# The order of issue on VectorE, ScalarE and GpSimd, taken from a list scheduler that reads a first trace

## The chip, the core and the metric

The kernel runs on one core of one Trainium2 chip. The metric is the device time of one execution in microseconds (us); a version's time is the median of its runs. The kernel before was run three times: 1061.58, 1067.97 and 1059.37 us, median 1061.58 us.

## The reference

A trunk of two layers on 256 tokens of width 1024, in float32. Each layer has a mixer and a feed-forward part, each followed by a residual sum and a layer norm:

```python
def _layer(x, ...):
    proj = x @ w_in                      # q, k, v, o, gates of branch A; q, k, v, z, gates of branch B; two merge gates
    ha = mlstm_chunked(qa, ka, va, ia, fa)           # 4 heads, exponential gates, running-max stabiliser
    ha = head_rmsnorm(ha) * sigmoid(oa)
    qb, kb, vb = split(silu(causal_conv(qkv_b, conv_w)))     # 4 taps
    hb = gated_delta_chunked(qb, kb, vb, beta, g)    # 8 heads, a unit lower triangular solve in each chunk
    hb = head_rmsnorm(hb) * silu(zb)
    y = sigmoid(gate_a) * (ha @ w_branch_a) + sigmoid(gate_b) * (hb @ w_branch_b)
    x = layernorm(ALPHA * x + y @ w_out)
    gt, up = split(x @ w_ffn_up)
    return layernorm(ALPHA * x + (silu(gt) * up) @ w_ffn_down)
```

## The kernel before

The large products are made from split numbers. A weight tile of 128 x 1024 is loaded to `raw` (three buffers, loads issued by SP, the SyncE queue); ScalarE (ACT) casts it to the high part `wH` (line 232), VectorE (DVE) subtracts to get the low part `wL` (line 233), and TensorE (PE) forms three products for each pair, `wH` x `xtH`, `wH` x `xtL` and `wL` x `xtH` (line 257). `wH` and `wL` have five buffers each, so ScalarE and VectorE can be a few tiles ahead of TensorE. There are some 320 tiles, and they give TensorE nearly all its work. The two numbers behind a tile's name in what follows only tell buffers of one name apart (`wH_876` is made from `raw_878`).

Between these products stand the small parts, all of which put work on VectorE and ScalarE: the gates (`gf`, line 431, to the rows `rw` that are written to DRAM and read back broadcast, lines 494 to 502 and 676), the causal convolutions (`cv`, `cu`, lines 622 to 637), the decay matrices (`KQ`, lines 667 to 725), the scores of branch A (copies `qk`, line 975, matmuls into a `sm` bank), the layer norms (lines 376 to 407) and the triangular solves. A solve is done four times, twice in a layer: VectorE transposes the 32 x 32 diagonal blocks into `Mt` (line 728), runs 31 steps of two operations (`tmp` and `stt`, lines 734 and 736), transposes the result into `t2` (line 740), ScalarE copies it in four pieces into `dm` (line 748), and TensorE multiplies with `dm`.

What sets the order: TensorE's is the order of the code (`manual_schedule` for PE), in which a plan, `PLAN`, tells after which weight tile (`U`) which small part takes its next step. The order of the other engines comes from the framework's own scheduler, by priorities from the place in the code; two places raise a priority by hand (lines 396 and 1027). Within an engine, instructions are issued in that order, and each waits for what it depends on; an instruction that isn't ready holds up those behind it.

Of the kernel before, what the change touches and what calls it, by code (L numbers as in the profile page):

```python
# [1 line left out]

# [8 lines left out]
F32 = mybir.dt.float32  # L11
# [7 lines left out]
NL = 2  # L19
# [111 lines left out]
class Net:  # L131
# [156 lines left out]
        return ps  # L288

    def splitA(self, xt, parts, done, pieces=1, order=None):  # L290
        """For each bank: how many units it has, and how many of them meet both halves of the tokens at once; the
        others meet the first half, and the second half after that of all banks. The last bank's second half is
        accumulated in so many pieces of its columns."""
        work = order or [(n, u) for n in range(len(parts)) for u in range(parts[n][0])]
        ps = {}
        held = []

        def second(n, u, units, us, which):
            cut = pieces if n == len(parts) - 1 else 1
            for i in which(cut):  # L300
                if u == 0:
                    ps[n, 1, i] = self.bank()
                cols = slice(i * 512 // cut, (i + 1) * 512 // cut)
                part = ps[n, 1, i][:, 0:512 // cut]
                self.partA(part, xt, us, u, 1, units - 1, cols=cols)
                if u == units - 1:
                    done(n, 1, part, cols)

        for n, u in work:
            units, both = parts[n]  # L310
            if u == 0:
                ps[n, 0] = self.bank()
            us = self.unit()
            self.partA(ps[n, 0], xt, us, u, 0, units - 1)
            if u < both:
                second(n, u, units, us, range)
                self.free(us)
                self.tick()
            else:
                held.append((n, u, units, us))  # L320
            self.tick()
            if u == units - 1:
                done(n, 0, ps[n, 0], slice(0, 512))
        for i in range(pieces):
            for n, u, units, us in held:
                second(n, u, units, us, lambda cut: (i,) if cut > 1 or i == 0 else ())
                if i == pieces - 1:
                    self.free(us)
                    self.fetch(min(len(self.ahead) + 1, 8))
                self.tick()  # L330
# [786 lines left out]
            self.F = None  # L1117


def program(arrays, dbg_shapes=None):  # L1120
    nc = bacc.Bacc("TRN2", target_bir_lowering=False, num_devices=1)
    a = {n: nc.dram_tensor("in_" + n, v.shape, mybir.dt.from_np(v.dtype), kind="ExternalInput").ap()
         for n, v in arrays.items()}
    out = nc.dram_tensor("out", (S, D), F32, kind="ExternalOutput").ap()
    dbg = None
    if dbg_shapes:
        dbg = {n: nc.dram_tensor("dbg_" + n, s, F32, kind="ExternalOutput").ap() for n, s in dbg_shapes.items()}
    with tile.TileContext(nc) as tc, ExitStack() as ctx:
        with tc.manual_schedule(engines={mybir.EngineType.PE}):
            Net(ctx, tc, a, dbg).run(out)  # L1130
    return nc


# [5 lines left out]
```

## Time and profile before

| | |
|---|---|
| runs | 1061.58, 1067.97, 1059.37 us (median 1061.58) |
| span of the profiled execution | 1058.5 us (only its span is given; the runs lie 0.9 to 9.5 us above it) |
| PE, PEld busy | 97%, 91% |
| DVE, ACT, POOL busy | 69%, 56%, 4% |
| granted TensorE clock, mean | 0.992 |
| chain that ended last | PE 71%, DMA 11%, DVE 8%, ACT 6%, issue 2%, POOL 1% |

PE is TensorE's matmul queue, PEld its weight loads, DVE VectorE, ACT ScalarE, POOL GpSimd, SP SyncE. Times in the views are microseconds from the start of the span. In a timeline, what stands in brackets is the time that the engine sat idle before the row, and what it then waited for. A granted clock of 1.00 is 2.4 GHz, one of 0.50 is 1.2 GHz.

### The profile page before, as it was taken

How to read it: one execution, taken by the hardware profiler on the slowest of the kernel's cores; microseconds unless marked ns; L12 is line 12 of the kernel's file. 1: busy time of each engine (PE TensorE's matmuls, PEld its weight loads, DVE VectorE, ACT ScalarE, POOL GpSimd, SP SyncE). 2: the span in 40 equal slices, each digit the busy share in tenths (PEclk: the TensorE clock that was granted, in tenths of full speed). 3: DMA queues.
4: the chain of work that ended last, by engine and by line, in shares of the span. 5: the costliest groups of instructions: out<-in, count | busy, mean ns of one | idle time of the engine just before them, and what ended most of it. 6: DMA issues, size and time to landing. Idle time of an engine off the chain costs nothing.

```text
span 1058.5 us, 18755 instructions
## 1 busy us (share of the span) xinstructions
PE 1030.0 (97%) x7378; PEld 959.5 (91%) x7378; DVE 730.0 (69%) x1309; ACT 596.7 (56%) x1106; POOL 42.5 (4%) x63
## 2 busy tenths in 40 slices
PE   8998999999999999999999989999999999999997
PEld 6897999989998799998788979999999978999886
DVE  5668976898658655655648598879985785555553
ACT  5567476757555544444535755667566654544441
POOL 0001000100000000000000100001000010000001
PEclk9999999999999999999999999999999999999999
DMA  7755525554456556666635564344544575666661
GB/s 243 260 182 183 170 87 160 159 179 140 140 179 217 178 175 191 197 196 200 221 106 182 159 220 140 119 144 156 161 151 145 183 242 156 185 196 197 188 211 41
DMA packets 57689, 183.62 MB, mean 173 GB/s; under 512 B 6656, under 2 KB 14336, under 8 KB 56960
## 3 DMA queue, kind: packets, MB, share of 16 engines
q1 hardware_dynamic: 50976, 179.13, 53.3%
q10 hardware_dynamic: 6624, 3.28, 1.2%
q8 instruction: 58, 0.95, 0.4%
q14 instruction: 31, 0.25, 0.1%
HBM read 181.21 MB, written 1.18 MB: 172 GB/s over the span
## 4 chain that ended last, share of the span: by engine, by line
PE 71%; DMA 11%; DVE 8%; ACT 6%; issue 2%; POOL 1%; SPq 0%; ACTq 0%; POOLq 0%; DVEq 0%
PE pj L257 61%; DMA raw<-in_ws 9%; PE sm L257 8%; DVE wL L233 3%; ACT wH L232 2%; DMA KQ<-rw 1%; PE sm L367 1%; DMA mr<-rw 1%; PE sm L647 1%; ACT wh L232 1%; DMA rw<-rt 1%; DVE wT L233 1%; POOL lnc L400 0%; DVE x L407 0%; DVE wh L233 0%
## 5 line engine op out<-in xcount | busy, mean ns | idle before, releaser
L233 DVE TENSOR_TENSOR wL<-raw,wH 128x1024 fp32r<-128x1024 f32 (+1 forms) x302 | 366.5, 1216 | 187.9 <-ACT wH L232 186.1
L232 ACT CAST wH<-raw 128x1024 fp32r<-128x1024 f32 (+1 forms) x302 | 315.3, 1046 | 266.5 <-PE pj L257 178.2
L257 PE MATMUL pj<-xtH,wH 128*128 128x256 f32 x1328 | 374.1, 282 | 1.5 <-ACT wH L232 1.5
L257 PE MATMUL pj<-xtH,wL 128*128 128x256 f32 x1328 | 368.9, 278 | 1.5 <-DVE wL L233 1.5
L257 PE MATMUL pj<-xtL,wH 128*128 128x256 f32 x1328 | 368.7, 278 | 0.0
L257 PEld LDWEIGHTS pj<-xtH,wH 128*128 128x128 f32 x1328 | 249.9, 188 | 2.1 <-ACT wH L232 1.9
L257 PEld LDWEIGHTS pj<-xtH,wL 128*128 128x128 f32 x1328 | 249.9, 188 | 2.0 <-DVE wL L233 1.9
L257 PEld LDWEIGHTS pj<-xtL,wH 128*128 128x128 f32 x1328 | 250.1, 188 | 0.1
L257 PE MATMUL pj<-wH,xtH 128*128 128x512 f32 x216 | 75.7, 412 | 2.6 <-ACT wH L232 2.6
L257 PE MATMUL pj<-wH,xtL 128*128 128x512 f32 x216 | 73.3, 400 | 0.0
L257 PE MATMUL pj<-wL,xtH 128*128 128x512 f32 x216 | 72.6, 397 | 0.1
L632 DVE SCALAR_TENSOR_TENSOR cv<-cu,cw,cv 128x255 f32<-128x255 f32 (+2 forms) x144 | 64.2, 480 | 7.3 <-ACT cv L630 6.8
L257 PE MATMUL pj<-wH,hH 128*128 128x512 f32 (+1 forms) x168 | 62.7, 373 | 0.0
L257 PE MATMUL pj<-wL,hH 128*128 128x512 f32 (+1 forms) x168 | 62.5, 372 | 0.0
L257 PE MATMUL pj<-wH,hL 128*128 128x512 f32 (+1 forms) x168 | 62.5, 372 | 0.0
L257 PEld LDWEIGHTS pj<-wH,xtL 128*128 128x128 f32 x216 | 41.7, 193 | 9.6
L257 PEld LDWEIGHTS pj<-wH,xtH 128*128 128x128 f32 x216 | 40.4, 194 | 10.9 <-ACT wH L232 3.5
L257 PEld LDWEIGHTS pj<-wL,xtH 128*128 128x128 f32 x216 | 41.5, 193 | 9.3 <-DVE wL L233 0.5
L734 DVE TENSOR_TENSOR tmp<-Mt,stt 128x248 f32<-128x248 f32 (+30 forms) x124 | 36.0, 290 | 1.7
L736 DVE TENSOR_TENSOR stt<-stt,tmp 128x248 f32<-128x248 f32 (+30 forms) x124 | 36.0, 290 | 1.7
L257 PEld LDWEIGHTS pj<-wH,hL 128*128 128x128 f32 x168 | 31.9, 190 | 5.5
L257 PEld LDWEIGHTS pj<-wH,hH 128*128 128x128 f32 x168 | 32.0, 190 | 5.3
(254 smaller groups left out, 1581.8 us busy)
## 6 DMA issues: line engine op xcount, KB each, us to landing
raw<-in_ws SPq DMA_DIRECT2D x322, 512.0 KB, 4.1
lnp<-in_ln SPq DMA_DIRECT2D x4, 1024.0 KB, 5.1
KQ<-rw ACTq DMA_DIRECT2D x8, 256.0 KB, 5.1
raw<-in_ws SPq DMA_DIRECT2D x4, 256.0 KB, 4.2
gn<-in_gn SPq DMA_DIRECT2D x2, 512.0 KB, 5.6
x<-in_x SPq DMA_DIRECT2D x1, 1024.0 KB, 8.2
mr<-rw ACTq DMA_DIRECT2D x4, 256.0 KB, 4.5
xraw<-in_xt SPq DMA_DIRECT2D x4, 128.0 KB, 3.1
```

What stands on the lines that cost most here:

```text
L232: nc.scalar.copy(out=h[:, sl], in_=r[:, sl])
L233: nc.vector.tensor_sub(out=lo[:, sl], in0=r[:, sl], in1=h[:, sl].bitcast(F32))
L257: self.nc.tensor.matmul(out, lhsT=l, rhs=r, start=start, stop=stop)
L367: self.nc.tensor.transpose(ps[:, i * P:(i + 1) * P], in_=src[:, i * P:(i + 1) * P], identity=self.idn)
L632: nc.vector.scalar_tensor_tensor(out=c[:, i, s:], in0=u[:, i, 0:S - s], scalar=cw[:, t, 3 - s:4 - s], in1=c[:, i, s:], op0=ALU.mult, op1=A ...
L647: self.nc.tensor.transpose(ps[:, h * P:h * P + P], in_=src[:, h, c * P:c * P + P], identity=self.idn)
L734: nc.vector.tensor_tensor(out=tmp[:, j + 1:, :], in0=mt[:, j + 1:, j:j + 1].to_broadcast([P, n, 8]), in1=stt[:, j:j + 1, :].to_broadcast([ ...
L736: nc.vector.tensor_tensor(out=stt[:, j + 1:, :], in0=stt[:, j + 1:, :], in1=tmp[:, j + 1:, :], op=ALU.subtract)
```

## The change

The program is traced twice. From the first trace `arrange` takes every instruction with its dependences, adds joins for tiles that share memory, gives each a cost from a formula for its engine and size (`cost`, nanoseconds), and works out for each the longest way to the end (`way`). Then it issues the instructions one by one: TensorE and SP in their old order, and on VectorE, ScalarE and GpSimd (`FREE`), of those ready within 150 ns of the first, the one with the longest way. In the second trace each engine of `FREE` gets that order as a chain of dependences without semaphores. What `Net` computes and the order of TensorE stay; a docstring and a debugging argument are dropped. Line numbers of `Net` rise by two.

```diff
+FREE = ("DVE", "Activation", "Pool")
+LOOK = 150
...
+def cost(i, engine, outs):
...
+    if op == "DMACopy":
+        return 330, 2100 + n * outs[0]["ap"][0][1] * 4 / 290
...
+    if engine == "DVE":
+        t = 150 + 1.04 * n * (2 if op == "StreamTranspose" else 1) + (60 if op == "TensorScalarPtr" else 0)
+    elif engine == "Activation":
+        t = 190 + 0.84 * n + (100 if scaled else 0) + (180 if len(outs) > 1 else 0)
+    else:
+        t = 300 + 0.4 * n if op == "Memset" else 900
+    return t - (0 if engine == "Pool" else 90), t + 35
...
+def arrange(nc, free):
...
+    for n in reversed(topological(along)):
+        way[n] = ops[n][4]
+        for m in along[n]:
+            soon = (n, m) in loose or m not in after[n] or ops[n][1] == ops[m][1] == "PE"
+            way[n] = max(way[n], ops[n][3 if soon else 4] + way[m])
...
+        for e, w in waiting.items():
+            if e in free:
+                if not w:
+                    continue
+                soon = min(max(now[e], ready[n]) for n in w)
+                n = max((n for n in w if max(now[e], ready[n]) <= soon + LOOK), key=lambda n: way[n])
+            else:
+                if at[e] == len(queue[e]) or queue[e][at[e]] not in w:
+                    continue
+                n = queue[e][at[e]]
...
+        if ops[n][0]["opcode"] == "DMACopy":
+            wire = max(start + 1200, wire) + ops[n][4] - 2100
+            when = wire + 900
...
-def program(arrays, dbg_shapes=None):
+def traced(arrays, order=None):
...
-            Net(ctx, tc, a, dbg).run(out)
+            Net(ctx, tc, a).run(out)
+        here = {i.name: i for i in nc.cur_bb.bb.instructions}
+        for names in (order or {}).values():
+            names = [n for n in names if n in here]
+            for x, y in zip(names, names[1:]):
+                tc.add_manual_dep(here[y], x, mybir.DependencyInfo(mybir.DependencyClass.NoSync, mybir.DependencyReason.DATA),
+                                  reason="order")
     return nc
+
+
+def program(arrays):
+    return traced(arrays, arrange(traced(arrays), FREE))
```

All three engines get another order: of VectorE's 1292 instructions 945 stand at another place, of ScalarE's 987 587, of GpSimd's 63 15. Three places are shown, each of before and then of the change.

ScalarE, layer 0, the copies `qk` of the score queries, which TensorE's score matmuls read. Before:

```order
L232 CAST wH_1205<-raw_1207 128x1024
L636 ACTIVATE cu_833<-cv_1198 128x512
L975 COPY qk_313<-pj_1022 128x512
L232 CAST wH_1229<-raw_1231 128x1024
L975 COPY qk_313<-pj_1023 128x512
```
Now:

```order
L234 CAST wH_1205<-raw_1207 128x1024
L632 ACTIVATE cv_1279<-cu_835,cw_98 128x256
L541 ACTIVATE wt_731<-wt_731,acol_539 128x128
L545 ACTIVATE wt_731<-wt_731,acol_539 128x128
L977 COPY qk_313<-pj_1022 128x512
L234 CAST wH_1229<-raw_1231 128x1024
L977 COPY qk_313<-pj_1023 128x512
```
The tanh of the convolution (`cu`, line 636 before) is no longer ahead of the copies; it stands 20 rows behind the first of them.

VectorE, layer 0, the second layer norm: `lnr` with `lnst` is the residual sum, `lnc` its coefficients, `x` the result, which TensorE transposes. Before:

```order
L233 TENSOR_TENSOR wT2_5710<-raw_5711,wT2_5710 128x1024
L233 TENSOR_TENSOR wT3_5741<-raw_5742,wT3_5741 128x1024
L376 SCALAR_TENSOR_TENSOR lnr_5561,lnst_5562<-x_77,pj_5569 128x512
L233 TENSOR_TENSOR wL_5753<-raw_5754,wH_5752 128x1024
L397 TENSOR_SCALAR lnc_5564<-lnst_5562,lnc_5564 128x1
L398 TENSOR_SCALAR lnc_5564<-lnst_5562 128x1
L399 SCALAR_TENSOR_TENSOR lnc_5564<-lnc_5564 128x1
L404 SCALAR_TENSOR_TENSOR lnr_5561<-lnr_5561,lnc_5564,lnp2_3811 128x512 x2
L407 SCALAR_TENSOR_TENSOR x_77<-lnr_5561,lnc_5564,lnp2_3811 128x512 x2
L233 TENSOR_TENSOR wL_5771<-raw_5772,wH_5770 128x1024
```
Now:

```order
L235 TENSOR_TENSOR wT2_5710<-raw_5711,wT2_5710 128x1024
L378 SCALAR_TENSOR_TENSOR lnr_5561,lnst_5562<-x_77,pj_5569 128x512
L399 TENSOR_SCALAR lnc_5564<-lnst_5562,lnc_5564 128x1
L401 SCALAR_TENSOR_TENSOR lnc_5564<-lnc_5564 128x1
L400 TENSOR_SCALAR lnc_5564<-lnst_5562 128x1
L406 SCALAR_TENSOR_TENSOR lnr_5561<-lnr_5561,lnc_5564,lnp2_3811 128x512 x2
L235 TENSOR_TENSOR wT3_5741<-raw_5742,wT3_5741 128x1024
L409 SCALAR_TENSOR_TENSOR x_77<-lnr_5561,lnc_5564,lnp2_3811 128x512 x2
L235 TENSOR_TENSOR wL_5753<-raw_5754,wH_5752 128x1024
```
The residual sum and the coefficients now stand ahead of the subtractions `wT3` and `wL_5753`.

ScalarE, layer 0, the copies `dg` of the diagonal blocks, from which VectorE's transpose `Mt` of the first solve is made (it stands behind `wL_907` on VectorE before, and behind `wL_1113` now). Before:

```order
L232 CAST wH_876<-raw_878 128x1024
L711 ACTIVATE KQ0_311<-sm_864,cc_747 128x128 x4
L232 CAST wH_906<-raw_908 128x1024
L724 COPY dg_936<-KQ0_311 32x256 x4
L232 CAST wH_954<-raw_956 128x1024
```
Now:

```order
L234 CAST wH_1024<-raw_1026 128x1024
L672 ACTIVATE KQ0_311<-KQ0_311,ngc_584 128x128 x4
L977 COPY qk_313<-pj_874 128x512
L234 CAST wH_1060<-raw_1062 128x1024
L977 COPY qk_313<-pj_875 128x512
L672 ACTIVATE KQ0_311<-KQ0_311,ngc_584 128x128 x3
L543 ACTIVATE wt_731<-mr_721,acol_539 128x128
L234 CAST wH_1112<-raw_1114 128x1024
L726 COPY dg_936<-KQ0_311 32x256 x4
```
`dg` has gone from behind the cast `wH_906` to behind `wH_1112`, five tiles later in the stream of weights.

On VectorE, fifteen subtractions `wL` stood between `Mt` and `t2` of the first solve of each layer, and nine do now; one `KQ` operation (line 667) and two `sg` operations of the same size (line 982) have left that piece too, and two small ones of line 570 have come. For the second solve of a layer it was thirteen and is nine, but six convolution steps (line 632) and two operations of line 637 have come.

## Rows read from the trace of the kernel before

**Rows 1.** The page: busy us of each engine, share of the span, instructions.
```profile
PE 1030.0 (97%) x7378; PEld 959.5 (91%) x7378; DVE 730.0 (69%) x1309; ACT 596.7 (56%) x1106; POOL 42.5 (4%) x63
```

**Rows 2.** Waits of PE from 16 us on: engine, line, releaser, total us, times, longest.
```profile
PE sm L257 <- ACT qk L975: 5.8, 2, 3.0
PE sm L367 <- DVE x L407: 5.7, 3, 2.4
PE pj L257 <- DVE wL L233: 1.5, 2, 0.8
PE pj L257 <- ACT wH L232: 1.5, 2, 1.1
PE sm L435 <- ACT gf L431: 1.4, 1, 1.4
PE sm L257 <- ACT vs L814: 0.7, 1, 0.7
PE sm L492 <- DVE lg L487: 0.3, 1, 0.3
```

**Rows 3.** Windows: stretch, us, busy per engine, granted clock, DMA share, GB/s.
```profile
102.70:109.50 6.80, 5.89 (x15) 4.74 (x16) 6.80 (x15) 3.34 (x5) 0.00 (x0) 0.50 0.60 192
529.40:532.80 3.40, 3.40 (x12) 2.71 (x11) 3.09 (x4) 1.55 (x3) 0.00 (x0) 0.50 0.55 160
624.90:628.40 3.50, 3.05 (x8) 2.58 (x9) 3.50 (x8) 2.88 (x4) 0.00 (x0) 0.51 0.58 206
373.00:495.00 122.00, 122.00 (x960) 117.43 (x961) 65.56 (x63) 56.68 (x63) 0.00 (x0) 1.00 0.61 189
86.00:135.40 49.40, 46.44 (x305) 42.68 (x305) 46.52 (x123) 26.22 (x44) 2.52 (x3) 0.93 0.59 185
```

**Rows 4.** Timeline of PE: start us, us, operation, idle before and its releaser.
```profile
81.03 0.28 PE L257 MATMUL pj<-xtL,wH 128*128 128x256 f32 x1
81.14 0.28 PE L257 MATMUL pj<-xtH,wL 128*128 128x256 f32 x1
82.47 0.38 PE L257 MATMUL pj<-xtH,wH 128*128 128x256 f32 x1 [1.05 <-ACT wH L232]
82.69 0.28 PE L257 MATMUL pj<-xtL,wH 128*128 128x256 f32 x1
```

**Rows 5.** Timeline of ACT around the score copies of layer 0.
```profile
96.36 1.05 ACT L232 CAST wH<-raw 128x1024 fp32r<-128x1024 f32 x1 [2.36 <-DMA raw<-in_ws]
101.51 1.04 ACT L232 CAST wH<-raw 128x1024 fp32r<-128x1024 f32 x1 [2.25 <-DVE wL L233]
102.47 0.62 ACT L636 ACTIVATE cu<-cv 128x512 f32<-128x512 f32 x1
103.00 0.56 ACT L975 COPY qk<-pj 128x512 f32<-128x512 f32 x1
```

**Rows 6.** Timeline of PE at the same place.
```profile
103.61 0.80 PE L257 MATMUL sm<-qk 128*128 128x256 f32 x1 [2.96 <-ACT qk L975]
```

**Rows 7.** Timeline of DVE at the second layer norm of layer 0.
```profile
521.48 1.23 DVE L233 TENSOR_TENSOR wT<-raw,wT 128x1024 fp32r<-128x1024 f32 x1 [1.42 <-ACT wT L232]
522.62 0.68 DVE L376 SCALAR_TENSOR_TENSOR lnr<-x,pj 128x512 f32<-128x512 f32 x1
523.63 1.23 DVE L233 TENSOR_TENSOR wL<-raw,wH 128x1024 fp32r<-128x1024 f32 x1 [0.32 <-ACT wH L232]
527.33 1.41 DVE L407 SCALAR_TENSOR_TENSOR x<-lnr,lnc,lnp 128x512 f32<-128x512 f32 x2 [0.76 <-POOL lnc L401]
```

**Rows 8.** Timeline of DVE at the end of the first triangular solve.
```profile
134.65 0.64 DVE L740 STREAM_TRANSPOSE t<-stt 128x256 f32<-128x256 f32 x1
```

**Rows 9.** Timeline of ACT right behind it.
```profile
135.38 2.77 ACT L748 COPY dm<-t 32x256 f32<-32x256 f32 x4 [2.57 <-DVE t L740]
```

**Rows 10.** Timeline of PE: the matmuls that read those copies.
```profile
141.73 1.06 PE L257 MATMUL sm<-kd,dm 128*128 128x128 f32 x8
```

**Rows 11.** The page's costliest groups: busy us, mean ns, idle before and its releaser.
```profile
L233 DVE TENSOR_TENSOR wL<-raw,wH 128x1024 fp32r<-128x1024 f32 (+1 forms) x302 | 366.5, 1216 | 187.9 <-ACT wH L232 186.1
```

**Rows 12.** Groups of DVE by line, same columns.
```profile
L667 DVE TENSOR_TENSOR KQ<-KQ,cst 128x512 f32<-128x512 f32 x8 | 5.5, 692 | 6.8 <-DMA KQ<-rw 3.9 <-ACT eg L663 2.9
```

**Rows 13.** The page's DMA issues: KB each, us from issue to landing.
```profile
raw<-in_ws SPq DMA_DIRECT2D x322, 512.0 KB, 4.1
KQ<-rw ACTq DMA_DIRECT2D x8, 256.0 KB, 5.1
```

More of the change, by code (lines that the diff above doesn't have):

```diff
@@ L1 @@
+import json
+import re
 from contextlib import ExitStack
@@ L1117, in run @@
             self.F = None
-def program(arrays, dbg_shapes=None):
+FREE = ("DVE", "Activation", "Pool")
+LOOK = 150
+STAGES = [p + str(l) for l in range(NL) for p in "MF"]
+def cost(i, engine, outs):
+    n = 1
+    for step in outs[0]["ap"][1:] if outs else ():
+        n *= step[1]
+    op = i["opcode"]
+    if op == "DMACopy":
+        return 330, 2100 + n * outs[0]["ap"][0][1] * 4 / 290
+    if op == "Matmult":
+        if i["ins"][0]["dtype"] == "float32r":
+            t = 113 * max(n, 128) / 256
+        else:
+            t = 109 * max(n, 64) / 128 if i.get("is_transpose") else 222 * max(n, 64) / 128
+        return t, t + 200
+    scaled = len([a for a in i["ins"] if isinstance(a, dict) and a.get("ap")]) > 1
+    if engine == "DVE":
[5 more added lines that the diff above has]
+    return t - (0 if engine == "Pool" else 90), t + 35
@@ new lines, in arrange, with release @@
+def arrange(nc, free):
+    nc.finalize()
+    program = json.loads(nc.to_json_bytes())
+    place, pool, queue = {}, {}, {}
+    ops = []
+    for f in program["functions"]:
+        for x in f["allocations"]:
+            for m in x.get("memorylocations") or []:
+                if m["type"] in ("SB", "PSUM"):
+                    at = m["addr"] + (2048 * m.get("bank", 0) if m["type"] == "PSUM" else 0)
+                    place[m["name"]] = (m["type"], at, at + m["dims"][1])
+                    pool[m["name"]] = m.get("ant_tile_pool_name")
+        for block in f["blocks"]:
+            for i in block["instructions"]:
+                if i["opcode"] not in ("EventSemaphore", "Drain", "UnconditionalBranch", "Call", "ISA", "LoadActFuncSet"):
+                    outs = [a for a in i.get("outs") or [] if isinstance(a, dict) and a.get("ap")]
+                    queue.setdefault(i["engine"], []).append(len(ops))
+                    ops.append((i, i["engine"], outs, *cost(i, i["engine"], outs)))
+    index = {o[0]["name"]: n for n, o in enumerate(ops)}
+    after = [set() for _ in ops]
+    loose = set()
+    for f in nc.python_module().functions:
+        for block in f.blocks:
+            for i in block.instructions:
+                if i.name in index:
+                    n = index[i.name]
+                    for kind, names in re.findall(r"(no_sync_)?deps=\[(.*?)\]", i.concise(deps=True)):
+                        for d in names.split(","):
+                            if d in index:
+                                after[index[d]].add(n)
+                                if kind:
+                                    loose.add((index[d], n))
+    users = {}
+    for n, (i, e, outs, *_) in enumerate(ops):
+        for a in list(i.get("ins") or []) + outs:
+            if isinstance(a, dict) and a.get("memref") in place:
+                users.setdefault(a["memref"], []).append(n)
+    step = replay(program)
+    begin = [step[o[0]["name"]] for o in ops]
+    held = {"SB": [], "PSUM": []}
+    for name in sorted(users, key=lambda t: min(begin[n] for n in users[t])):
+        space, lo, hi = place[name]
+        old = [t for t in held[space] if t[0] < hi and lo < t[1]]
+        held[space] = [t for t in held[space] if not (lo <= t[0] and t[1] <= hi)] + [(lo, hi, name)]
+        if old:
+            join = len(ops)
+            ops.append((None, None, (), 0, 0))
+            after.append(set(users[name]))
+            for _, _, t in old:
+                for n in users[t]:
+                    after[n].add(join)
+    stages = [sorted({n for t in users if pool[t] == p for n in users[t]}) for p in STAGES]
+    for old, new in zip(stages, stages[1:]):
+        join = len(ops)
+        ops.append((None, None, (), 0, 0))
+        after.append(set(new) - set(old))
+        for n in old:
+            after[n].add(join)
+            loose.add((n, join))
+    way = [0.0] * len(ops)
+    along = [list(s) for s in after]
+    for e, q in queue.items():
+        if e not in free:
+            for x, y in zip(q, q[1:]):
+                along[x].append(y)
+    for n in reversed(topological(along)):
[3 more added lines that the diff above has]
+            way[n] = max(way[n], ops[n][3 if soon else 4] + way[m])
+    left = [0] * len(ops)
+    for s in after:
+        for m in s:
+            left[m] += 1
+    ready = [0.0] * len(ops)
+    now = dict.fromkeys(queue, 0.0)
+    waiting = {e: [] for e in queue}
+    at = dict.fromkeys(queue, 0)
+    order = {e: [] for e in queue}
+    wire = 0.0
+    def release(n, when, issued):
+        for m in after[n]:
+            left[m] -= 1
+            if (n, m) not in loose:
+                ready[m] = max(ready[m], issued if ops[m][1] == ops[n][1] == "PE" else when)
+            if left[m] == 0:
+                if ops[m][0] is None:
+                    release(m, ready[m], ready[m])
+                else:
+                    waiting[ops[m][1]].append(m)
+    for n, o in enumerate(ops):
+        if o[0] is not None and left[n] == 0:
+            waiting[o[1]].append(n)
+    while True:
+        best = None
+        for e, w in waiting.items():
[4 more added lines that the diff above has]
+                n = max((n for n in w if max(now[e], ready[n]) <= soon + LOOK), key=lambda n: way[n])
+            else:
+                if at[e] == len(queue[e]) or queue[e][at[e]] not in w:
+                    continue
+                n = queue[e][at[e]]
+            start = max(now[e], ready[n])
+            if best is None or start < best[0]:
+                best = start, e, n
+        if best is None:
+            break
+        start, e, n = best
+        waiting[e].remove(n)
+        order[e].append(ops[n][0]["name"])
+        at[e] += 1
+        now[e] = start + ops[n][3]
+        when = start + ops[n][4]
+        if ops[n][0]["opcode"] == "DMACopy":
+            wire = max(start + 1200, wire) + ops[n][4] - 2100
+            when = wire + 900
+        release(n, when, now[e])
+    return {e: order[e] for e in free}
@@ new lines, in topological, with replay @@
+def topological(after):
+    left = [0] * len(after)
+    for s in after:
+        for m in s:
+            left[m] += 1
+    out = [n for n, k in enumerate(left) if k == 0]
+    for n in out:
+        for m in after[n]:
+            left[m] -= 1
+            if left[m] == 0:
+                out.append(m)
+    assert len(out) == len(after), "the order has a cycle"
+    return out
+def replay(program):
+    queue, count, turn = {}, {}, {}
+    for f in program["functions"]:
+        for block in f["blocks"]:
+            for i in block["instructions"]:
+                sync = i.get("sync_info") or {}
+                queue.setdefault(i["engine"], []).append((i["name"], sync.get("on_wait") or [], sync.get("on_update") or []))
+    at = dict.fromkeys(queue, 0)
+    more = True
+    while more:
+        more = False
+        for e, q in queue.items():
+            while at[e] < len(q):
+                name, waits, updates = q[at[e]]
+                if any("barrier" not in w["ant_name"] and count.get(w["id"], 0) < w["wait_value"] for w in waits):
+                    break
+                for u in updates:
+                    count[u["id"]] = count.get(u["id"], 0) + u["update_value"]
+                turn[name] = len(turn)
+                at[e] += 1
+                more = True
+    return turn
@@ L1124, in program @@
     out = nc.dram_tensor("out", (S, D), F32, kind="ExternalOutput").ap()
-    dbg = None
-    if dbg_shapes:
-        dbg = {n: nc.dram_tensor("dbg_" + n, s, F32, kind="ExternalOutput").ap() for n, s in dbg_shapes.items()}
     with tile.TileContext(nc) as tc, ExitStack() as ctx:
         with tc.manual_schedule(engines={mybir.EngineType.PE}):
-            Net(ctx, tc, a, dbg).run(out)
-    return nc
+            Net(ctx, tc, a).run(out)
[5 more added lines that the diff above has]
+                                  reason="order")
+    return nc
+def program(arrays):
+    return traced(arrays, arrange(traced(arrays), FREE))
 def kernel(**inputs):
```

## The prediction

> **What bounds the kernel now.** The page comes first [rows 1]: TensorE's matmuls are busy 97% of the span, its weight loads 91%, VectorE 69%, ScalarE 56%. TensorE's order is left as it is and its work too, so all that another order on the other engines can give is the time in which TensorE waits for them. Second I read what TensorE waits for, from 16 us on, behind the first loads [rows 2]. There are twelve waits: two for the score copies `qk` (5.8 us), three for the layer norm's `x` (5.7), two each for `wL` and `wH` (1.5 and 1.5), one each for the gates `gf` (1.4), the solve's `vs` (0.7) and `lg` (0.3): 16.9 us. Third, I read the windows [rows 3]. In the feed-forward stretch 373 to 495 there is no idle time at a granted clock of 1.00, so nothing is to be had there. Behind three of the long waits the granted clock is 0.50, half speed: behind the `qk` wait of each layer and behind the `x` wait of layer 0's second norm.
>
> Two timelines show what ended these waits. At 103 us TensorE stood idle 2.96 us [rows 6] for a copy `qk` of 0.56 us, of matmuls that had all ended when the idle time began; on ScalarE it stood behind the cast at 101.51, which waited 2.25 us, and a tanh [rows 5]. At 521 us the residual sum of the layer norm stood behind `wT` at 521.48, which had itself waited 1.42 us for its cast, and its coefficients behind `wL` at 523.63; `x` came at 527.33 [rows 7]. In both a small operation waits in a queue behind a weight operation that nobody needs yet. These waits are a matter of order, which is what the change changes.
>
> **What goes.** In all of the twelve the order of the change takes the small operation ahead, or the weight operation where that was late.
> - The idle time itself: 16.9 us.
> - Restart: idle time is counted from the modelled end of a matmul, though the next one would start before it. At 82 us the starts are 81.03, 81.14, 82.47 and 82.69 [rows 4]: the first two, where nothing waits, lie 0.11 us apart, the last three took 1.55 us for two such steps, so 1.33 us were lost against 1.05 counted. Behind a longer matmul the difference is smaller; I take 0.2 us for each of the twelve, 2.4 us.
> - Half clock: TensorE is busy 5.89 + 3.40 + 3.05 = 12.3 us at 0.50 [rows 3]; at full speed this is half of it. 6.2 us. It goes if the waits ahead of it go.
>
> Together 25.5 us. Two shares of it matter below. In layer 0 the scores hold 2.96 + 0.2 + 2.9 = 6.1 us and the two weight waits at 82 us 1.1 + 0.8 + 0.4 = 2.3 us: some 8.3 us between 81 us and the solve's matmuls. In layer 1 the same waits hold 2.8 + 0.2 + 1.5 and 0.4 + 0.7 + 0.4: 6.0 us.
>
> **What comes.** TensorE then arrives earlier everywhere, and what it arrives at must be earlier too. Where I find the least room is the first solve. Its transpose `t` ended at 135.29 [rows 8], the four copies `dm` took until 138.15 [rows 9], and TensorE read them at 141.73 [rows 10], with room of 3.6 us. With 8.3 us less ahead of it, TensorE is there at 133.4 us on the same axis. VectorE was busy 46.52 of 49.4 us from 86 to 135.4 [rows 3], so the solve is bound by VectorE. By the order it loses six `wL` of 1.22 us [rows 11] and three operations of 0.69 us [rows 12] from that piece and gets two of some 0.2 us: 46.5 - 7.3 - 2.1 + 0.4 = 37.5 us, or 40.4 with the same 2.9 us idle. Against that it begins later, since `dg` now stands behind the cast of `wH_1112`. That cast was at 96.36 in the profile, when its load landed [rows 5]. Late end: it stays there; then it ends at 97.4, four copies `dg` of 0.4 us bring 99.0, 40.4 us of VectorE 139.4, and 2.8 us of copies 142.2, so that TensorE waits 8.8 us. Early end: the chain of loads allows it. Three `raw` buffers mean that this load starts when the subtraction three tiles before ends. Counted from the end of `wL_877`, which at the latest is wanted at some 81.4 us, it takes a load of 4.1 us [rows 13], a cast of 1.05, a subtraction of 1.2, again a load: 91.9 us and a wait of 4.4. `wL_877` can be several microseconds earlier than wanted, since now neither the squares nor the scalings stand ahead of its cast; with five microseconds there is no wait. So 0 to 8.8 us; I take 2.5, nearer to the early end, because the order moves just those casts and subtractions ahead. In layer 1 TensorE gains 2 us less and the solve is the same: I take 1.0. At the second solves thirteen `wL` have become nine, which pays for the convolution that came: nothing, within 0 to 2 us each. The six row loads (`KQ`, `mr`) that now go out together, 5.1 us each [rows 13], are wanted some ten microseconds after they are issued: nothing, but 1.5 MB of them beside the loads of weights could cost a load, 0 to 3 us. On GpSimd fifteen instructions move by four places at most: nothing.
>
> **The sum.** 1058.5 - 25.5 + 3.5 = 1036.5 us of span. The runs lay 0.9 to 9.5 us above the span of the profile, the median 3.1. On that footing 1039.6, in round numbers 1040 us.
>
> A rule speaks to how much there can be. The Trainium skill, Perfetto Trace Analysis, Identifying the Most-Contended Engine, says that matmul busy time tells little of the distance to the roofline, and that the busy share of the weight loads should be taken. By the 91% there would be 9% or 99 us of headroom where the matmul row leaves 28.5. The trace puts both in proportion: the stretch that has no wait at all holds weight loads for 117.43 of 122.00 us, 96% [rows 3], so a kernel without a wait would show about that, and most of the 9% isn't headroom of the order. I keep to the 25.5 us from waits and clock.
>
> **The rivals.**
> - *The solves give it back.* VectorE is the second bound: if the first solve of each layer ends no sooner than now, TensorE stands at `dm` for all that it gained before, 8.3 and 6.0 us, in place of my 3.5. 1040 + 14.3 - 3.5 = 1051, and with a microsecond at the second solves 1052. For it: 94% busy, and `cost` gives a copy `dm` half of its 0.68 us and a row load less than its 5.1. Against: nine operations fewer in the piece. The gain at the norms and the gates, 11 us, stays.
> - *Slower: the solves come late and the clock falls.* Waits of 2.96 and 2.43 us were followed by half speed, the first by 5.9 us of it. If each of the four `dm` waits is as long as my late end, 8.8 us, each costs 0.2 of restart and 2.9 of half clock on top, 11.9 in all: 1061.6 - 25.5 + 47.6 = 1084. It decides from 6.4 us a place, where the gain is used up; at 9 us a place it is over 1% slower. Against: the late end asks that the load of `wH_1112` gain nothing though the tiles ahead of it go first.
> - *The loads come late.* If the row loads together hold up the weights, TensorE waits at the next tiles, 3 us a layer and restart: 1046 us.
> - *The change doesn't do what it says*, because a wait holds the old order in place: 1061. The order that is shown speaks against it.
>
> **Chances.** Forecast 0.68, its own range 1034 to 1048. The solves give it back 0.14, half of it under 1051 and half over. Slower 0.06, in which anything between 1072 and 1084. Loads late 0.09, still faster. No effect 0.03. One per cent, 10.6 us, is about what can be told from no change here: faster is below 1051, slower above 1072. Faster 0.68 + 0.09 + 0.07 = 0.84, of which I take 0.03 off for a slow fit of several small waits that no row shows: 0.81; same 0.13; slower 0.06. The range: nothing given back and the lowest run's distance of 0.9 us is 1034; upwards it takes in the late loads and most of the solves' case: 1033 to 1055.
>
> **What would show it.** The waits of TensorE should list `qk`, `x`, `gf` and `lg` with a few tenths each, and no stretch of half clock from 16 us to the last norm. A new row would be TensorE waiting for `dm` of line 750, at about 131 us of the new span, and its twin in layer 1; its size is the term that I am least sure of. On VectorE the first solve should take about 40 us from `Mt` to `t` in place of 49. The prediction is wrong if `dm` waits of over 4 us stand there, or if weight waits (`wH`, `wL`) show up in number in the mixer where now there are four.

## The result and the profile after

Timed beside the kernel before, the changed kernel took 1046.67 us (median of four runs, 1044.89 to 1049.60) against 1062.32 us: ratio 0.984, 95% interval 0.980 to 0.988, so 1.6% faster (the two medians alone stand at 0.985). The profiled execution, the fastest of the four, has a span of 1043.1 us, 15.4 us under the 1058.5 of before. The forecast was 1040 us with a range of 1033 to 1055: faster by over 1%, as was held likeliest, and 6.7 us less of it.

The page's first line of the changed kernel, as [rows 1]:

```profile
PE 1023.2 (98%) x7378; PEld 956.2 (92%) x7378; DVE 739.9 (71%) x1309; ACT 602.0 (58%) x1106; POOL 42.4 (4%) x63
```

TensorE's matmuls are 6.8 us less busy, though they are the same ones. Most of that is half clock that went: before, the three windows of [rows 3] held 13.7 us at half speed; now there is one such stretch of some 3.4 us, which makes some 5 us less. All that TensorE waits for from 16 us on, as [rows 2]:

```profile
PE sm L259 <- ACT dm L750: 7.1, 4, 3.2
PE sm L649 <- DVE ha L582: 0.6, 1, 0.6
PE sm L1081 <- DVE fhA L1076: 0.5, 1, 0.5
PE pj L259 <- DVE yL L1037: 0.4, 2, 0.2
```

None of the twelve waits of before is left, nor a thirteenth of 0.2 us (`wh`, line 233) that the list of before holds and [rows 2] leaves out. In their place stand 8.6 us of new ones, 7.1 of them for `dm`, the copies behind the triangular solves, which were no row of that list before. The two places that were read closely went as the order says. ScalarE at the score copies (as [rows 5]) issues them with nothing late ahead of them:

```profile
93.97 0.56 ACT L977 COPY qk<-pj 128x512 f32<-128x512 f32 x1
94.43 1.04 ACT L234 CAST wH<-raw 128x1024 fp32r<-128x1024 f32 x1
95.38 0.57 ACT L977 COPY qk<-pj 128x512 f32<-128x512 f32 x1
```

and VectorE at the second layer norm of layer 0 (as [rows 7]) has the residual sum right behind `wT2`, and `wT3` in the place where it waited 0.76 us for GpSimd before:

```profile
513.07 1.23 DVE L235 TENSOR_TENSOR wT<-raw,wT 128x1024 fp32r<-128x1024 f32 x1 [0.42 <-ACT wT L234]
514.21 0.68 DVE L378 SCALAR_TENSOR_TENSOR lnr<-x,pj 128x512 f32<-128x512 f32 x1
515.57 1.42 DVE L406 SCALAR_TENSOR_TENSOR lnr<-lnr,lnc,lnp 128x512 f32<-128x512 f32 x2
516.91 1.21 DVE L235 TENSOR_TENSOR wT<-raw,wT 128x1024 fp32r<-128x1024 f32 x1
518.04 1.40 DVE L409 SCALAR_TENSOR_TENSOR x<-lnr,lnc,lnp 128x512 f32<-128x512 f32 x2
```

The new wait is seen at the end of the first solve. VectorE, ScalarE and TensorE (as [rows 8, 9, 10]):

```profile
131.79 0.17 DVE L738 TENSOR_TENSOR stt<-stt,tmp 128x8 f32<-128x8 f32 x1
132.13 0.63 DVE L742 STREAM_TRANSPOSE t<-stt 128x256 f32<-128x256 f32 x1
```

```profile
132.79 2.62 ACT L750 COPY dm<-t 32x256 f32<-32x256 f32 x4 [2.77 <-DVE dd L573]
```

```profile
132.07 0.28 PE L259 MATMUL pj<-xtH,wL 128*128 128x256 f32 x1
135.47 2.08 PE L259 MATMUL sm<-kd,dm 128*128 128x128 f32 x8 [3.12 <-ACT dm L750]
```

The transpose `t` ended at 132.76, the copies at 135.41; TensorE had run out of work at 132.35 and began at 135.47. Before, the same copies were done 3.6 us ahead of TensorE. Windows, as [rows 3], of the first solve from `Mt` to `t` and of the time behind the wait:

```profile
89.30:132.80 43.50, 42.45 (x292) 39.08 (x290) 41.55 (x117) 24.74 (x55) 1.73 (x3) 1.00 0.40 123
135.40:139.00 3.60, 3.53 (x17) 3.54 (x18) 2.78 (x4) 1.64 (x3) 0.00 (x0) 0.53 0.21 43
```

The solve has VectorE busy for 41.55 of 43.50 us, and behind the wait TensorE ran at a granted clock of 0.53 for 3.6 us.

TensorE's matmuls are the same and in the same order in both, so each can be put beside its twin; the difference of their starts says where time went (worked out from the two traces, us):

| up to | later (+) or earlier (-) than before | change in this piece |
|---|---|---|
| gates and the two weights at 82 us | -4.6 | -4.6 |
| scores of layer 0 and the half clock behind | -10.5 | -5.9 |
| first solve of layer 0 | -4.6 | +5.9 |
| second solve, output projection | -3.5 | +1.0 |
| first norm of layer 0 | -6.0 | -2.5 |
| feed-forward, second norm | -9.6 | -3.6 |
| weights and scores of layer 1 | -16.5 | -6.9 |
| its first solve | -14.5 | +2.0 |
| its second solve, output projection | -13.3 | +1.2 |
| its first norm, to the end | -15.4 | -2.1 |

25.6 us were gained and 10.1 given back. Of the first 4.6, 0.6 lie in the first loads, ahead of 16 us. Of the 5.9 at the first solve of layer 0, 4.2 lie ahead of the first matmul that reads `dm` and 1.7 behind it, where the clock was at half speed.

### The profile page after: what moved, and what is told of

Read it like the earlier page. It is cut to its first block, busy times and chain, and to the rows that moved or that the text cites. A ratio compares the mean times of both kernels' runs of the same rounds, so it can differ in the third digit from the quotient of the medians.

```text
span 1043.1 us, 18734 instructions
## 1 busy us (share of the span) xinstructions
PE 1023.2 (98%) x7378; PEld 956.2 (92%) x7378; DVE 739.9 (71%) x1309; ACT 602.0 (58%) x1106; POOL 42.4 (4%) x63
## 4 chain that ended last, share of the span: by engine, by line
PE 88%; DVE 7%; ACT 2%; DMA 1%; issue 1%; SPq 0%; POOL 0%; POOLq 0%; DVEq 0%; ACTq 0%
PE pj L259 78%; PE sm L259 8%; DVE wL L235 2%; DMA raw<-in_ws 1%; DVE stt L738 1%; PE sm L369 1%; DVE tmp L736 1%; ACT dm L750 1%; DVE cv L634 1%; PE sm L649 1%; ACT wH L234 0%; DVE ha L582 0%; DVE wt L553 0%; DVE yL L1037 0%; DVE vT L639 0%
## 5 line engine op out<-in xcount | busy, mean ns | idle before, releaser
L634 DVE SCALAR_TENSOR_TENSOR cv<-cu,cw,cv 128x255 f32<-128x255 f32 (+2 forms) x144 | 60.4, 476 | 1.0 <-ACT cv L632 0.9
L259 PEld LDWEIGHTS pj<-wL,hH 128*128 128x128 f32 x168 | 31.7, 189 | 5.3
```

The source lines that it names most:

```text
L259: self.nc.tensor.matmul(out, lhsT=l, rhs=r, start=start, stop=stop)
L634: nc.vector.scalar_tensor_tensor(out=c[:, i, s:], in0=u[:, i, 0:S - s], scalar=cw[:, t, 3 - s:4 - s], in1=c[:, i, s:], op0=ALU.mult, op1=A ...
```

## The experiments

Each is a small edit of the changed kernel. "Before" beside it is the kernel before on the same chip; its medians were 1061.3 to 1063.5 us. Spans are of one profiled execution each, and two of them can stand a microsecond or two apart already behind the first loads; so where it matters, TensorE's matmuls are put beside their twins in the changed kernel.

### One engine alone given to the scheduler

```diff
-FREE = ("DVE", "Activation", "Pool")
+FREE = ("DVE",)
```

> Only VectorE takes the scheduler's order; ScalarE and GpSimd keep the framework's. Theory (each wait belongs to the queue in which the small operation stood): the three waits for the layer norm's x (5.7 us, 1.7 us of half clock) and lg (0.3) go, the waits for qk (5.8 us, with 4.4 us of half clock) and gf (1.4) stay: span some 8 to 9 us under the 1058.5 of before, about 1050. Rival (the two queues only gain together, since each waits for the other's casts and subtractions): within 3 us of 1058.5.

1057.43 us, ratio 0.993 (0.991 to 0.996), span 1056.7 us, of which 3.5 us are slow matmuls that have nothing to do with the order (last section): 1053.2 without. What TensorE waited for:

```profile
PE sm L259 <- DVE sq L577: 3.1, 2, 1.8
PE sm L369 <- DVE x L409: 2.9, 3, 1.6
PE pj L259 <- DVE wL L235: 2.6, 2, 1.7
...
```

The waits for `x` are halved and those for `qk` fall to 1.8 us, but weights, `sq` and `ha` (2.6 us) came in. The 1053.2 lie between the two expectations, and neither describes the run.

```diff
+FREE = ("Activation",)
```

> Only ScalarE takes the scheduler's order; VectorE and GpSimd keep the framework's. Theory: the waits for qk and gf go (5.8 + 1.4 us, 4.4 us of half clock), those for x stay (5.7 us), and since the solve on VectorE is no shorter than before, a wait for dm of 2 us or more comes up in each layer: span 1048 to 1052. Rival (no new wait at dm without the new order on VectorE): under 1047.

1061.90 us, ratio 1.001 (0.998 to 1.004), span 1058.4 us. Here too the first waits:

```profile
PE sm L369 <- DVE x L409: 6.0, 3, 2.2
PE sm L259 <- DVE lg L474: 4.7, 1, 4.7
PE sm L259 <- ACT qk L977: 2.5, 2, 1.6
...
```

`gf` is gone, `qk` more than halved and `x` stays; `dm` costs 1.0 us in all and not 2 in each layer, and `lg`, on VectorE, costs 4.7 us in one wait. The span is outside both expectations. VectorE's order, though, is not that of before. There the last steps that lead to `lg` stood one right behind another:

```profile
45.94 1.48 DVE L464 SCALAR_TENSOR_TENSOR gP<-gP,gS 128x24 f32<-128x24 f32 x7
```

In this run convolution steps and subtractions stand between them, and `lg` comes at 54.05 us in place of 48.04:

```profile
50.64 0.47 DVE L634 SCALAR_TENSOR_TENSOR cv<-cu,cw,cv 128x253 f32<-128x253 f32 x1
51.12 1.22 DVE L235 TENSOR_TENSOR wL<-raw,wH 128x1024 fp32r<-128x1024 f32 x1
54.05 0.16 DVE L474 TENSOR_TENSOR lg<-gP,nea 128x16 f32<-128x16 f32 x1
```

The engine that the edit leaves to the framework gets another order too. By the traces (operation and tile, buffer numbers aside) 489 of VectorE's 1309 instructions start at another place here than before, and in the run ahead of this one 258 of ScalarE's 1106. Nor is the freed engine's order the changed kernel's, since the scheduler makes it anew with the others' old order in its model: 759 of VectorE's 1309 places differ. So these two runs hold no engine still, and whether each wait belongs to the queue in which the small operation stood stays open. What they show is less: one engine given to the scheduler alone gained 5.3 and 0.1 us of span, all three together 15.4.

### The score copies late again

```diff
+    for k in (2, 6):
+        at = [n for n, x in enumerate(q) if made.get(x, "").startswith("wH_") and n > q.index(copies[k])][1]
...
+        q[q.index(late) + 1:q.index(late) + 1] = copies[k:k + 2]
```

> The changed kernel, with the two score copies qk of each layer put behind the second cast that followed them, so that TensorE waits there again, some 2.5 us, perhaps with half clock behind it (2.9 us more). Theory (the first solve is the bound behind the scores): the wait for dm that comes later shrinks by as much, and the span stays within 2 us of 1043.1. Rival (the waits are independent and add up): 5 to 11 us longer, 1048 to 1054, the dm waits as they were (3.1 and 3.2 us).

1052.64 us, ratio 0.991 (0.988 to 0.995), span 1054.3 us, 1050.8 without the slow matmuls: 7.7 us longer. VectorE's order is the changed kernel's throughout.

```profile
PE sm L259 <- ACT dm L750: 7.1, 4, 3.2
PE sm L259 <- ACT qk L977: 4.1, 2, 2.9
...
```

TensorE waits 4.1 us for `qk`, runs at half clock behind the first of the two waits (0.55 from 100.5 to 104.0 us), and still waits 7.1 us for `dm`. Put beside its twins, it is 1.1 us later behind the first loads, where no `qk` is at work, 4.2 more at the scores of layer 0 and 1.5 at those of layer 1; the first solve of layer 0 takes back 0.5, and that of layer 1 adds 1.5. The rival holds: the waits add up. The gain at the scores is not taken back by a solve that ends when it always did; the solve comes later too. VectorE's timeline shows how, between steps of the solve:

```profile
100.56 0.56 DVE L553 SCALAR_TENSOR_TENSOR wt<-sm,wt 128x384 f32<-128x384 f32 x1 [0.89 <-PE sm L259]
...
105.44 1.22 DVE L235 TENSOR_TENSOR wL<-raw,wH 128x1024 fp32r<-128x1024 f32 x1 [1.26 <-PE sm L259]
```

In its queue between the steps stand an operation that reads the scores themselves (`wt`) and a subtraction, and both waited for TensorE, so a late TensorE stops VectorE. From `Mt` to `t` the solve took 46.5 us, 3.1 more; VectorE waits 2.4 us in this piece, and in the changed kernel it has no such wait. The room between them hardly depends on how early TensorE is.

### The solve shortened

```diff
         for j in range(31):
             n = 31 - j
-            nc.vector.tensor_tensor(out=tmp[:, j + 1:, :], ...
-            nc.vector.tensor_tensor(out=stt[:, j + 1:, :], ...
+            if j < 23:
+                nc.vector.tensor_tensor(out=tmp[:, j + 1:, :], ...
+                nc.vector.tensor_tensor(out=stt[:, j + 1:, :], ...
```

> The changed kernel with the last eight of the 31 steps of each solve left out (so its output isn't the reference's): sixteen short operations of some 0.22 us less, 3.5 us, with the same other work between the first and the last step. Theory (the dm wait is what the solve ends too late, and the half clock behind it hangs on it): no wait for dm over 0.3 us, no half clock at the solves, TensorE 5 to 6 us earlier behind the first solve of layer 0 and 2.5 to 3.5 behind that of layer 1, 0.4 at each second solve: span 1034 to 1036. Rival (other work that TensorE wants there, vT, ha or a weight, is as late as dm): TensorE gains under half of that, span 1039 to 1043.

1037.28 us, ratio 0.977 (0.974 to 0.981), span 1035.9 us.

```profile
PE sm L259 <- ACT dm L751: 1.9, 2, 1.3
...
```

7.2 us of span for 2.4 to 3.1 us less from `Mt` to `t` in each of the four solves; `dm` waits fall from 7.1 to 1.9 us, and the clock stays at full speed behind them. (Behind the first loads, at 15.1 us, this execution ran at half clock for 3.4 us, which put all that follows some 1.7 us later.) Beside its twins TensorE gains 4.5 us at the first solve of layer 0, 2.8 at that of layer 1 and 0.7 at each second solve: the theory, a little short at the first, where 1.3 us of wait were left against its 0.3. Most of what was given back hangs on the solves' length.

### More weight on what leads to `dm`

```diff
+        if outs and outs[0]["memref"].startswith("dm"):
+            t = 680
...
+        due = 3000 if ops[n][2] and ops[n][2][0].get("memref", "").startswith("dm") else 0
...
-            way[n] = max(way[n], ops[n][3 if soon else 4] + way[m])
+            way[n] = max(way[n], ops[n][3 if soon else 4] + way[m] + due)
```

> The changed kernel; the scheduler prices the copies dm at the 680 ns that the profile shows, and adds 3 us to the way of what leads to dm, so that the solve is put ahead of other work sooner. Theory (the order leaves the solve too little room, VectorE has it earlier on): the first dm waits of both layers fall from 3.1 and 3.2 us to under 1 us, and the span to about 1036 to 1039. Rival (VectorE is full ahead of dm, whatever the order): the sum of TensorE's waits stays within 1.5 us, and other waits (vT, ha, wL) take the place: span 1041 to 1045.

1046.18 us, ratio 0.985 (0.979 to 0.992), span 1041.6 us.

```profile
PE sm L649 <- DVE ha L582: 2.6, 2, 1.3
PE sm L649 <- ACT vs L816: 2.5, 2, 1.2
PE pj L259 <- DVE yL L1037: 1.1, 2, 0.9
PE sm L259 <- DVE wt L553: 0.9, 1, 0.9
PE sm L369 <- DVE x L409: 0.3, 1, 0.3
```

No wait for `dm` any more, and 7.4 us for others that want VectorE and ScalarE in the same stretch, against 8.6 in all in the changed kernel. The rival holds: an order within that stretch only picks who waits. The half clock moved with them: it now stands in both layers behind the waits for `ha` and `vs`, each of 1.2 to 1.3 us. The first of the two windows (as [rows 3]):

```profile
128.10:131.50 3.40, 3.40 (x19) 3.40 (x18) 3.19 (x12) 2.58 (x7) 0.00 (x0) 0.50 0.52 154
```

### Fewer row loads at once

In the changed kernel six row loads go out together from ScalarE's queue. Its timeline (ACTq is the queue's issuing):

```profile
59.50 2.62 ACTq L678 DMA_DIRECT2D KQ<-rw  x3
62.16 0.21 ACT L488 ACTIVATE kde<-kde 128x8 f32<-128x8 f32 x1 [2.58 <-issue]
62.19 2.81 ACTq L678 DMA_DIRECT2D KQ<-rw  x1
65.04 1.05 ACT L234 CAST wH<-raw 128x1024 fp32r<-128x1024 f32 x1 [2.67 <-issue]
```

The issues held ScalarE twice for 2.6 us, and VectorE's next subtraction, at 66.13, waited 3.6 us for its cast. The edit adds a dependence that keeps the last two behind the cast that they followed before:

```diff
+        if ops[n][0]["opcode"] == "DMACopy" and ops[n][2][0]["memref"].startswith("KQ1"):
+            c = next(m for m in reversed(q[:p]) if ops[m][2] and ops[m][2][0]["memref"].startswith("wH_"))
+            after[c].add(n)
+            loose.add((c, n))
```

> The changed kernel, with the two row loads of KQ1 of each layer kept behind the cast that they followed in the kernel before, so that four row loads go out together and not six. In the changed kernel ScalarE stood 2.6 and 2.7 us at the fifth and sixth issue in layer 0 and 2 us in layer 1, VectorE 3.6 us behind it. Theory (these microseconds of VectorE are what the first solve lacks): the dm wait of layer 0 falls from 3.1 us to under 0.5, that of layer 1 from 3.2 to about 2, and the half clock behind the first goes: span 1036 to 1039. Rival (VectorE would idle at another place ahead of the solve, for want of a free buffer): dm waits within 0.7 us of the old, span 1042 to 1044.

1049.68 us, ratio 0.987 (0.975 to 0.999), span 1045.8 us.

```profile
PE sm L259 <- ACT dm L750: 7.1, 4, 3.2
...
```

The rival holds: the same waits for `dm`, and 0.7 us more for `ha`. The span is above its range, 2.7 us longer than the changed kernel's, mostly by clock: beside its twins TensorE is 0.8 us later behind the first loads and loses 1.5 us at the first solve of layer 1, where the granted clock is 0.80 and 0.70 over some 3 us and 1.00 in the changed kernel. Time that VectorE gets at 62 us is of no use to a solve that begins at 89. With both edits in one:

> Both in one: the row loads of KQ1 kept late, and 3 us added to the way of what leads to dm, with dm priced at 680 ns. Theory (VectorE lacks 3.6 us ahead of the solve; with them there is room for the solve and the convolution): no dm wait over 0.5 us and the waits for ha, vs and wt together under 3 us, span 1034 to 1037. Rival (VectorE stays full): waits of 6 to 8 us in all as with the 3 us alone, span 1040 to 1043.

1046.71 us, ratio 0.984 (0.972 to 0.996), span 1043.9 us, 0.9 above the rival's range, and 7.8 us of waits: the rival again.

### Filling the gaps of the solve

```diff
-LOOK = 150
+LOOK = 100
```

> The changed kernel with LOOK = 100 in place of 150, so that a step of the solve that becomes ready 125 ns after its predecessor could be overtaken: 54 of the 63 gaps between the steps of the first solve are filled with other work, and 19 before. A dependent step starts 34 ns after its predecessor ends, an independent one 85 ns before. Theory (what counts is the room on VectorE, and a filled gap saves 0.12 us): 35 gaps save some 4 us of VectorE, the dm waits of the first solves fall under 1 us, span 1035 to 1040. Rival (what counts is what is put ahead of the solve; thirteen wL in the piece instead of nine lengthen it by 4 to 5 us): dm waits of 4 us and more, span 1046 to 1054.

1059.48 us, ratio 0.998 (0.995 to 1.001), span 1057.6 us.

```profile
PE sm L259 <- ACT dm L750: 17.2, 4, 5.8
...
```

A miss of the theory; the rival named what happened, and by more than it said (its span ended at 1054). 54 gaps of the first solve were filled, and the pieces from `Mt` to `t` became 44.6, 44.3, 47.8 and 44.3 us long where the changed kernel has 43.4, 38.4, 43.7 and 38.4. In the first piece the durations grew by 6.7 us, of which the filled gaps took back 5.5; in the second solves only five more gaps were filled, and five more `wL` of 1.2 us stand in the piece. A filled gap saves 0.12 us, and each `wL` that came made these solves over a microsecond longer. With the row loads late as well:

> Both in one: the row loads of KQ1 kept late, and LOOK = 100. Theory of room: the smallest waits of all, under 4 us from 16 us on, span 1033 to 1037. Rival (overtaking puts weight tiles ahead of the solve): longer than with the row loads alone.

1065.91 us, ratio 1.003 (0.999 to 1.006), span 1067.4 us, of which 3.5 us slow matmuls; 22.0 us of `dm` waits: the rival.

### The solve begun earlier

On top of the late row loads, 20 us are added to the way of what leads to `Mt`:

```diff
+        due = 20000 if ops[n][2] and ops[n][2][0].get("memref", "").startswith("Mt") else 0
```

> The row loads of KQ1 kept late, and 20 us added in the scheduler to the way of whatever leads to Mt, so that each solve begins two or three weight tiles sooner (Mt behind wL_1025, not wL_1113, in layer 0); the order within the solve is left to the rule. Eleven wL stand in the first piece, nine before. Theory (the first solve starts late because ScalarE and VectorE put work ahead of dg and Mt that isn't due): Mt some 4 us earlier, the piece some 2 us longer, dm wait of layer 0 and 1 down from 3.1 and 3.2 to about 1 us, span 1037 to 1040. Rival (what is put behind Mt is missed elsewhere, VectorE and ScalarE being full): waits for wH, wL or qk take its place, span 1042 to 1047.

1041.61 us, ratio 0.982 (0.977 to 0.986), span 1038.3 us.

```profile
PE sm L259 <- ACT dm L750: 5.6, 4, 2.5
...
```

`Mt` starts at 84.1 us, 5.2 earlier, the piece is 3.0 us longer, and the waits fall as the theory says, if less: 2.5 and 2.3 us are left at the first solves, and no half clock behind them. Then the same with 1.5 us for `dm` and its price, and with 40 us and 2 us:

```diff
+        due = 20000 if made.startswith("Mt") else 1500 if made.startswith("dm") else 0
```

> The row loads of KQ1 kept late, 20 us added to the way of what leads to Mt, 1.5 us to that of what leads to dm, and dm priced at 680 ns. Theory (VectorE's room ahead of the second copies dm is shared by the solve and the convolution; begun early, both can be in time): dm waits of the first solves from 2.5 us to 1 us or less, waits for vT, ha, vs and wt together under 1.5 us, span 1035 to 1038. Rival (the room is used up): what dm gains the others lose, span 1038 to 1040.

1040.28 us, ratio 0.980 (0.976 to 0.985), span 1038.2 us: `dm` waits 1.3 us at each first solve, `ha` 0.9, but 2.3 us for `yH` and `yL` at the output projections, which the expectation did not name. The rival by its number, though it named other places.

> The same with 40 us for Mt and 2 us for dm: dg and Mt stand where they stood in the kernel before, behind wH_906 and wL_907, with fourteen wL in the first piece. Theory of room: TensorE's waits from 16 us on in all no larger than with 20 us and 1.5 us, span 1034 to 1038. Rival (Mt this early takes ScalarE and VectorE from the casts and subtractions at 82 us, which waited in the kernel before): waits for wH and wL of 1 us or more come back there, span 1038 to 1041.

1039.87 us, ratio 0.980 (0.976 to 0.984), span 1035.1 us, the lowest of all versions that leave nothing out.

```profile
PE sm L259 <- ACT dm L750: 1.5, 2, 0.8
PE pj L259 <- DVE yL L1037: 1.1, 2, 0.9
PE sm L649 <- DVE ha L582: 0.9, 2, 0.5
...
```

The theory of room holds by the waits, 3.9 us in all against 6.4: `Mt` at 79.0 us, the casts at 82 us don't suffer. Put beside its twins, TensorE ends 8.0 us before the changed kernel, 1.0 of it gained ahead of the scores and 1.7 by half clock that is no more. The span is that of the fastest of five runs (1037.18 to 1044.11 us); by the runs this version can't be told from the two ahead of it. The intervals against the changed kernel (0.976 to 0.984, and 0.980 to 0.988) overlap at the edge, so what the runs alone say is: probably faster by some 0.4%.

## Why the prediction was right, and what was off

- **What goes: right.** Twelve waits, half clock and restart were put at 25.5 us; 25.6 us were gained before what came. By places, forecast and measured: up to 82 us 4.4 and 4.6 (0.6 of it in the first loads, of which the forecast said nothing), scores of layer 0 6.1 and 5.9, its two norms 5.9 and 6.1, weights and scores of layer 1 6.0 and 6.9, its first norm 2.1 and 2.1; the wait for `vs`, 0.9, lies within the first solve of layer 1, which the table gives net. That late copies were the cause is shown by an edit for `qk` alone; for `x`, `gf` and the weights it rests on the order, the lists of waits and the twins.
- **What comes: right in its place, wrong in its size.** 3.5 us were forecast, 2.5 and 1.0 at the first solves; 10.1 came: 5.9 and 2.0 at the first solves, 2.2 behind them.
- **The step that failed** is "46.5 - 7.3 - 2.1 + 0.4 = 37.5 us, or 40.4 with the same 2.9 us idle". It took durations off busy time; the piece took 43.4 us. On VectorE durations overlap. Before, an operation that doesn't need its neighbour starts 0.08 us before that one ends:

```profile
98.58 0.39 DVE L736 TENSOR_TENSOR stt<-stt,tmp 128x224 f32<-128x224 f32 x1
98.89 0.48 DVE L632 SCALAR_TENSOR_TENSOR cv<-cu,cw,cv 128x255 f32<-128x255 f32 x1
99.28 0.38 DVE L734 TENSOR_TENSOR tmp<-Mt,stt 128x216 f32<-128x216 f32 x1
```

where in the changed kernel steps stand one behind the other, and each starts 0.03 to 0.04 us after its predecessor:

```profile
126.21 0.24 DVE L736 TENSOR_TENSOR tmp<-Mt,stt 128x80 f32<-128x80 f32 x1
126.49 0.24 DVE L738 TENSOR_TENSOR stt<-stt,tmp 128x80 f32<-128x80 f32 x1
126.77 0.23 DVE L736 TENSOR_TENSOR tmp<-Mt,stt 128x72 f32<-128x72 f32 x1
```

Of the 63 gaps between the steps of the first solve 54 held other work before, and 19 now. Added up over the piece: 55.75 us of durations before, 46.37 now, 9.4 less where 9.0 were forecast; but 9.3 us of overlap have become 4.9, and 0.3 us of gaps between steps have become 1.9. That takes 6.1 us of the 9.4 back; 2.5 us of waits for ScalarE and GpSimd inside the piece, which I had left in as idle time, went. 49.2 became 43.4, not 40.4.
- **The clock behind the wait** was counted among what goes and in the slower rival, not in the 2.5 us: 3.6 us at 0.53 are 1.7 us. The sign "no stretch of half clock" did not come out.
- **The start of the solve** was a guess within nearly 9 us, and luck: 2.5 us of wait mean `Mt` at 133.4 + 2.5 - 2.8 - 40.4 = 92.7 us on the prediction's axis, which is 90.3 in the new trace, since 2.4 us were gained ahead of 79 us. `Mt` began at 89.3, and this microsecond hid a third of the 3.0 us by which the piece was too short in the forecast.
- **Row loads and second solves at nothing.** The prediction bounded what the row loads could cost the loads of weights and named no hold of ScalarE; their issue held it for 5.2 us in layer 0. It cost no time that shows: with two of the six kept late, the waits for `dm` were the same. The second solves and the projections cost 2.2 us in place of nothing, within 0 to 2 each.
- **The rival in which the solves give it back** was right in its place. Its mechanism, a solve that ends no sooner, isn't what happens: `t` ended at 132.76 us and not at 135.29, and the late copies showed that the waits add up.

Not tried: the same order on a solve with fewer steps that still computes the reference.

## What to carry to other kernels

Waits of the bounding engine for small operations that stand behind work not yet due can be summed from the list of waits, with the half clock behind them; here the new order gave 25.6 us where that sum was 25.5. What it gives back is decided where a second engine is full: count its time there from starts to starts, not from durations, and ask when its chain can begin, for an order inside a full stretch only picks who waits. And to free one engine does not hold the others still: here the framework gave them another order as well, so compare the order of every engine before a run is read as a test of one.

## What the runs showed of the hardware

Three of the fourteen profiled executions (with VectorE's order alone, with the late copies, and with late row loads and LOOK = 100) had a stretch of some 800 matmuls that started 0.118 us apart in place of 0.113, 3.5 us longer, in the feed-forward part, without a wait and at a granted clock of 1.00. The late copies, and then the changed kernel, over 60 us of the same matmuls (as [rows 3]):

```profile
395.00:455.00 60.00, 60.00 (x512) 60.00 (x511) 32.18 (x31) 28.24 (x32) 0.00 (x0) 1.00 0.60 186
```

```profile
390.00:450.00 60.00, 60.00 (x532) 60.00 (x531) 33.40 (x32) 28.90 (x33) 0.00 (x0) 1.00 0.63 194
```

512 matmuls against 532. The granted clock doesn't show it; the count in a stretch without waits does. What causes it stays open. Shorter runs of matmuls 0.118 us apart stand in the mixers of all fourteen executions, some 1100 to 1700 matmuls in each that lacks the long stretch. And a wait of 3.12 us at the first solve was followed by half clock (0.53 over 3.6 us), while behind the wait of 2.5 us at the same place, with the solve begun earlier, the granted clock is 1.00. Behind equal waits it differs too: the 3.2 us at the first solve of layer 1 were followed by 1.00 in the changed kernel, and by 0.70 with the row loads late. Nor does the single longest wait order these cases: with more weight on `dm`, where no wait there was over 1.3 us, the granted clock behind two of them was 0.50.
